# Decoder layer on one core: logits of two pairs of heads taken in one visit, in three places

## The chip, the cores and the metric

The kernel runs on one core of a Trainium2 chip. The engines are TensorE (PE in the profile), VectorE (DVE), ScalarE (ACT) and GpSimd (POOL); SyncE (SP) issues most of the DMAs. The metric is device time in microseconds, the median of several runs. All arithmetic that ends in the output is float32.

## The reference, cut to what matters

One layer of a decoder over 256 positions of width 1024. Three token mixers work side by side on projections of the same input, each with heads of 64:

```python
# A, 6 heads: sparse attention, one shared key and value; an indexer picks the top 64 keys of each query
logits = jnp.einsum('bqhd,bqkd->bqhk', qb, ksel) * scale + bias
# B, 3 groups x 4 slots: dilated windows; 3 query groups share a slot's keys, merged by their denominators
logits = jnp.einsum('bqhd,bqjhd->bqhj', qb[:, :, g], kg) * scale + bias
# C, 6 heads: block-sparse causal attention (with 256 positions: one causal block)
# all: softmax over the allowed keys, then the weighted sum of values
m = sum_b sigmoid(x @ Wg_b) * (o_b @ P_b)
x = LN(alpha * x + m @ w_out)
x = LN(alpha * x + relu(x @ w_up)**2 @ w_down + sigmoid(x @ w_ple_gate) * (p @ w_ple))
```

A table of relative-position biases is added to all logits.

## The kernel before

**Products.** A float32 product is made of three TensorE products of parts rounded to fp32r: high by high, high by low, low by high (`prod`, L184 to L192). Activations are split once; `xh` and `xl` are the parts of the input. Weights stream through `Weights` (L80 to L140): SP loads a unit into one of five `raw` buffers, ACT casts it to its high part `whi` (L112), DVE and POOL subtract to get the low part `wlo` (L123, each a share of the columns). Units are prepared four ahead of their use (`AHEAD`), in the order of the table `TASKS` (L44): a number is a feature tile, `g` a gate tile, `c` a merged output, `va` and `vb` the values, `a` and `o` what follows behind the mixers.

**Steps of the mixers.** `feat(f)` makes a tile of 128 projected features by 256 positions with 24 matmuls in one of three PSUM banks called `mm`; `q_pair` (ACT L285, DVE L286) and `k_pair` (L298, L299) read it, scale it and split it, which frees the bank. A tile of 128 features holds a pair of heads. `fill("g")` makes a gate tile in an `mm` bank, 24 matmuls, and ACT's tanh (L311, output `G`) frees the bank. `fill("c")` makes the merged output of mixers B and C for 128 columns with 15 matmuls from `op`, the heads' outputs (B gives its tiles 3 and 4, C its tiles 5 to 7), and three operations of DVE (L326, L326, L327) gate it and free the bank.

**Attention.** `logits` (L336 to L351) is one visit: for the two heads of a pair 12 matmuls with 64 rows, or 24 where a second pair rides along. Its results lie in the PSUM banks b0, b1, b2, taken in turn by `ps_s`; a 24-visit takes b3 too, through `ps_t`. `head` (L411 to L422) then does one head: DVE adds the bias (L416, output `e`, with the row minimum), ACT takes exp with the row sums (L419), DVE the reciprocal (L406), ACT the scaling by rows (L408, two instructions), and `attend` (L382 to L398) does the rest: three transposes on PE into b3 (L388), an ACT copy and a DVE subtraction into `pt` (L389, L390), two matmuls with the values into b4 (L392, L393), an ACT copy `ov` (L396) and two DVE additions (L397, L398). `pair_out` (ACT L401, DVE L402) splits a pair's output into `op`. `slots` does mixer B's pairs in the same manner, for three query groups at once.

**Order.** The mixers run as a series: two dilated pairs (`slots`, the first with a 24-visit for two of its three groups, the second with three 12-visits), three causal pairs (loop at L557), three query pairs of branch a (loop at L573, with the key `kA` shared by all heads), then what follows. Feature, gate and merged tiles stand between the heads. The scheduler writes one order for each engine from this program, and each engine executes its instructions strictly in that order; logits have a high priority in it (L341). The tiles for `e` come from the pool `wk` with three buffers, and branch a's masked bias `ta` (POOL, L584 and L585) from the same pool.

Of the kernel before, what the change touches and what calls it, by code (L numbers as in the profile page):

```python
# [11 lines left out]
F32 = mybir.dt.float32  # L12
# [28 lines left out]
DV = 640  # L41


TASKS = ("4 va 5 g 6 7 g 8 g g 9 g 10 11 g 12 g g vb g 13 14 g g 15 16 g g 17 18 g g "  # L44
         "19 g c 20 g c g c 21 g c g c g c g g g c c a a a a o o o o").split()


class Apart:
# [95 lines left out]
def hybrid_layer(ctx: ExitStack, tc: tile.TileContext, x0, xn, pT, wqk, wva, wvb, wg, wbc, wba,  # L144
# [188 lines left out]
            next(side, None)  # L333
        return ps

    def logits(k, *qs):  # L336


        ss = [next(ps_s if n < 3 else ps_t)[:, 0:384] for n in range(2 * len(qs))]
        with tc.high_priority(offset=500):  # L340
            for b in range(2):  # L341
                c = slice(b * 128, (b + 1) * 128)
                for n, q in enumerate(qs):
                    for i, (x, y) in enumerate(((1, 0), (0, 0), (0, 1))):
                        for h in (1, 0):
                            d = slice(64 * h, 64 * h + 64)
                            m = pe.matmul(ss[2 * n + h][:, QC[b]], lhsT=q[d, x, c],  # L347
                                          rhs=k[d, y, 0:128 * (b + 1)], start=i == 0, stop=i == 2)
# [59 lines left out]
            act.mul(P[:, QC[b]], P[:, QC[b]], r[:, b:b + 1])  # L408


    def head(s, t0, t1, vh, o, h):  # L411
        e = wk.tile([128, 384], F32, name="e", tag="e")
        mx = sm.tile([128, 2], F32, name="mx", tag="mx")
        den = sm.tile([128, 2], F32, name="den", tag="den")
        for b, t in enumerate((t0, t1)):
            dve.tensor_tensor_reduce(e[:, QC[b]], s[h][:, QC[b]], t, op0=ALU.add, op1=ALU.min,  # L416
                                     scale=1.0, scalar=-GONE, accum_out=mx[:, b:b + 1])
        for b in range(2):
            act.activation(e[:, QC[b]], e[:, QC[b]], AF.Exp, bias=mx[:, b:b + 1], scale=-1.0,  # L419
                           accum_out=den[:, b:b + 1])  # L420
        scale_rows(e, den)
        attend(e, vh, o, h)  # L422

    def slots(qs, k, Ts, vh, o, adds, two):

        es = [wk2.tile([128, 3, 384], F32, name="eb", tag="eb") for _ in range(2)]
        mxs = [sm.tile([128, 2, 3], F32, name="mxb", tag="mxb") for _ in range(2)]
        for g in range(3):

            if two and g == 0:  # L430
                s = logits(k, qs[1], qs[0])
                s, ss = s[2:], s[:2]
            else:
                s = ss if two and g == 1 else logits(k, qs[g])
# [33 lines left out]
    with ExitStack() as begin:  # L468
# [26 lines left out]
    tp, wk, wk2, sm = (right(n, b) for n, b in (("tp", 3), ("wk", 3), ("wk2", 2), ("sm", 6)))  # L495
    tab = bias_table()
    ps = feat(4)
    kI, kA = k_pair(ps[0:64], ps[0:64]), k_pair(ps[64:128], ps[64:128])
# [7 lines left out]

    values(u_va, 328, 0, 5, True)
    for j in range(4):
        s = s[2:] if j % 2 else logits(kI, iq[j], iq[j + 1])
# [23 lines left out]
    def opair():  # L533
        return wk2.tile([128, S], F32, name="o", tag="o")

    for j in range(2):
        ps = feat(5 + 4 * j)
        k = k_pair(ps)
        fill("g")
        qs = []  # L540
        for g in range(3):
            qs.append(q_pair(feat(6 + 4 * j + g)))
            if g:
                fill("g")
        o = opair()
        Ts = [toeplitz(6 + 2 * j + h, 4) for h in range(2)]
        slots(qs, k, Ts, 1 + 2 * j, o, (pool, dve)[j], j == 0)
        pair_out(o, 3 + j)
        banks_first[0] = True
        fill("g")  # L550
# [3 lines left out]
    dve.tensor_tensor(pl, pr, ph.bitcast(F32), op=ALU.subtract)  # L554
    values(u_vb, 384, 5, 6, False)
    fill("g")
    for j in range(3):  # L557
        ps = feat(13 + 2 * j)
        k = k_pair(ps)
        q = q_pair(feat(14 + 2 * j))  # L560
        s = logits(k, q)
        o = opair()
        for h in range(2):
            n = 2 * j + h
            if n % 3 == 0:
                T = toeplitz(18 + n, 1)
            head(s, T[:, n % 3, 128:256], T[:, n % 3], 5 + n, o, h)
            fill("g")
        pair_out(o, 5 + j)

    for _ in side:
        pass
    T = None  # L573
    q = q_pair(feat(19))
    for j in range(3):
        s = logits(kA, q)
        o = opair()
        for h in range(2):
            n = 2 * j + h
            if n % 3 == 0:  # L580
                T = toeplitz(n, 1)
            ta = wk.tile([128, 384], F32, name="ta", tag="ta")
            with tc.issue_after(W.subs[-3]):
                pool.tensor_tensor(ta[:, 0:128], T[:, n % 3, 128:256], am[:, 0:128], op=ALU.add)  # L584
                pool.tensor_tensor(ta[:, 128:384], T[:, n % 3], am[:, 128:384], op=ALU.add)  # L585
            head(s, ta[:, 0:128], ta[:, 128:384], 0, o, h)
            if h and j < 2:
                q = q_pair(feat(20 + j))
            fill("gc")
        pair_out(o, j)  # L590
    fill("gggcc")
    W.after = ()

# [532 lines left out]
```

## Time and profile before

| what | value |
|---|---|
| median of three runs | 429.45 us (429.26 to 430.65) |
| the profiled execution: its own time | 428.66 us |
| its span in the trace | 426.9 us |
| mean granted TensorE clock | 0.998 |
| 24-visits and 12-visits of the mixers at L347 | from 46 us to 165 us of the span |
| DVE busy, POOL busy | 82%, 28% |
| moved by DMA | 84.30 MB, 197 GB/s in the mean |

The span is what the trace covers; the execution's own time is 1.8 us longer. Times in rows of the trace count from the start of the span. In a row, `out<-in` names the tiles with their buffer numbers left out, and `x24` is the number of instructions in the group. The page cuts the span into 40 slices and gives each engine's busy share in tenths:

```profile
DVE  5968758898676689879967889989998798999755
ACT  6777385585888777858414668887888666567310
POOL 1668474173544556500010002242220000000001
```

A slice is 10.7 us; the mixers' attention fills slices 5 to 16. Busy shares of a slice say nothing of the order within it.

### The profile page before, as it was taken

What the parts mean: (1) busy time and instruction counts of PE and PEld (TensorE: products, weight loads), DVE (VectorE), ACT (ScalarE), POOL (GpSimd) and SP (SyncE); (2) the same over time, 40 slices, a digit from 0 to 9 for tenths busy, and PEclk for the clock granted to TensorE, in tenths of its full rate; (3) what the DMA queues carried; (4) which work ended last, traced back from release to release, by engine and by line L of the source; (5) the groups of instructions that cost most, each with busy time, mean ns of one, the idle gap of its engine ahead of it and who ended that gap; (6) DMA issues with size and microseconds to landing.
All of it is one profiled execution on the core that took longest, in us unless ns stands there. A gap on an engine that the chain in (4) does not pass through costs nothing.

```text
span 426.9 us, 7810 instructions
## 1 busy us (share of the span) xinstructions
PE 417.1 (98%) x2804; PEld 378.1 (89%) x2804; DVE 351.1 (82%) x645; ACT 279.6 (65%) x531; POOL 118.9 (28%) x127
## 2 busy tenths in 40 slices
PE   8999999999999999999999999999999999999993
PEld 8989999999999999999887888888888888788883
DVE  5968758898676689879967889989998798999755
ACT  6777385585888777858414668887888666567310
POOL 1668474173544556500010002242220000000001
PEclk9999999999999999999999999999999999999999
DMA  8895966567463327587851776785665376646402
GB/s 294 301 327 161 286 222 189 164 201 269 130 181 126 131 63 259 145 267 276 292 206 49 236 257 197 210 291 191 187 207 152 117 266 216 190 147 230 164 2 99
DMA packets 28157, 84.30 MB, mean 197 GB/s; under 512 B 2977, under 2 KB 6985, under 8 KB 27733
## 3 DMA queue, kind: packets, MB, share of 16 engines
q1 hardware_dynamic: 26880, 79.54, 57.0%
q10 hardware_dynamic: 1140, 4.19, 2.8%
q8 instruction: 22, 0.36, 0.4%
q14 instruction: 19, 0.15, 0.1%
q0 software_dynamic: 96, 0.06, 0.0%
HBM read 81.88 MB, written 1.90 MB: 196 GB/s over the span
## 4 chain that ended last, share of the span: by engine, by line
PE 78%; DVE 5%; DMA 4%; issue 2%; ACT 2%; SPq 0%; POOLq 0%; DVEq 0%; POOL 0%; ACTq 0%
PE mm L189 34%; PE b L189 19%; PE mm L891 14%; PE mm L893 7%; DMA xr<-in_wdn_dram 4%; PE b L347 2%; DVE wlo L119 2%; PE b L388 1%; PE b L392 1%; ACT whi L112 1%; DVE Y L853 1%; ACT ri L517 1%; PE b L393 0%; DVE wlo L123 0%; DVE st L701 0%
## 5 line engine op out<-in xcount | busy, mean ns | idle before, releaser
L112 ACT CAST whi<-raw 128x1024 fp32r<-128x1024 f32 (+3 forms) x92 | 89.9, 988 | 38.2 <-PE b L189 14.7
L123 DVE TENSOR_TENSOR wlo<-raw,whi 128x256 fp32r<-128x256 f32 (+3 forms) x118 | 96.4, 840 | 16.6 <-ACT whi L112 13.9
L189 PE MATMUL mm<-xh,whi 128*128 128x256 f32 x336 | 90.2, 280 | 0.0
L189 PE MATMUL mm<-xl,whi 128*128 128x256 f32 x336 | 88.1, 278 | 0.0
L123 POOL TENSOR_TENSOR wlo<-raw,whi 128x384 fp32r<-128x384 f32 (+1 forms) x50 | 68.4, 1377 | 70.2 <-ACT whi L112 65.5
L189 PE MATMUL mm<-xh,wlo 128*128 128x256 f32 x336 | 80.6, 281 | 0.2 <-DVE k L299 0.2
L189 PEld LDWEIGHTS mm<-xh,whi 128*128 128x128 f32 x336 | 63.1, 188 | 0.8
L891 PE MATMUL mm<-x,whi 128*128 128x512 f32 x256 | 63.4, 389 | 0.0
L189 PEld LDWEIGHTS mm<-xl,whi 128*128 128x128 f32 x336 | 63.1, 188 | 0.1
L189 PEld LDWEIGHTS mm<-xh,wlo 128*128 128x128 f32 x336 | 57.8, 188 | 0.8 <-DVE k L299 0.4
L189 PE MATMUL b<-whi,store 128*128 128x512 f32 x168 | 54.1, 389 | 0.0
L891 PEld LDWEIGHTS mm<-x,whi 128*128 128x128 f32 x256 | 45.7, 188 | 7.5
L119 DVE TENSOR_TENSOR wlo<-raw,whi 128x1024 fp32r<-128x1024 f32 (+2 forms) x38 | 43.2, 1159 | 3.7 <-ACT whi L112 3.6
L708 POOL TENSOR_TENSOR rs<-rs,half 128x1 f32<-128x1 f32 x4 | 3.4, 843 | 147.5 <-DVE rs L707 147.5
L110 ACT CAST whi<-raw 128x256 fp32r<-128x256 f32 x64 | 36.9, 617 | 10.0 <-PE mm L891 5.4
L189 PEld LDWEIGHTS b<-whi,store 128*128 128x128 f32 x168 | 31.5, 188 | 6.4
L893 PEld LDWEIGHTS mm<-x,wlo 128*128 128x128 f32 x256 | 33.8, 188 | 2.5
L893 PE MATMUL mm<-x,wlo 128*128 128x256 f32 x256 | 34.2, 276 | 0.0
L189 PE MATMUL b<-wlo,store 128*128 128x512 f32 x84 | 32.8, 391 | 0.3 <-DVE wlo L119 0.3
L914 POOL TENSOR_TENSOR a<-a 128x128 f32<-128x128 f32 x7 | 5.3, 757 | 61.5 <-ACT a L877 55.6
L189 PE MATMUL mm<-op,whi 128*128 128x256 f32 x128 | 22.4, 280 | 0.0
L189 PE MATMUL b<-whi,x 128*128 128x512 f32 x64 | 20.5, 395 | 0.0
(223 smaller groups left out, 824.2 us busy)
## 6 DMA issues: line engine op xcount, KB each, us to landing
raw<-in_wup_dram SPq DMA_DIRECT2D x32, 512.0 KB
raw<-in_wg_dram SPq DMA_DIRECT2D x24, 512.0 KB
raw<-in_wqk_dram SPq DMA_DIRECT2D x18, 512.0 KB
raw<-in_wdn_dram SPq DMA_DIRECT2D x18, 512.0 KB
raw<-in_wout_dram SPq DMA_DIRECT2D x8, 512.0 KB
raw<-in_wpg_dram SPq DMA_DIRECT2D x8, 512.0 KB
T<-tabd SPq DMA_DIRECT2D x24, 128.0 KB
xr<-in_wdn_dram SPq DMA_DIRECT2D x6, 512.0 KB
```

The source lines that it names most:

```text
L110: i = nc.scalar.copy(blocks(hi, a, b), blocks(r, a, b))
L112: i = nc.scalar.copy(hi, r)
L119: i = e.tensor_tensor(lo[:, x], r[:, x], hi[:, x].bitcast(F32), op=ALU.subtract)
L123: i = e.tensor_tensor(blocks(lo, *x), blocks(r, *x), blocks(hi, *x).bitcast(F32), op=ALU.subtract)
L189: i = pe.matmul(ps, lhsT=a[x], rhs=b[y], start=first and n == 0, stop=last and n == 2, skip_group_check=more)
L347: m = pe.matmul(ss[2 * n + h][:, QC[b]], lhsT=q[d, x, c], rhs=k[d, y, 0:128 * (b + 1)], start=i == 0, stop=i == 2)
L388: pe.transpose(t[:, 128 * i:128 * i + 128], P[:, 128 * i:128 * i + 128], ident)
L392: pe.matmul(v, lhsT=V[:, 0, vh], rhs=pt[:, :, 0:256], start=True, stop=False)
L517: act.mul(r[:, h, QC[0]], r[:, h, QC[0]], iw[:, 0, n:n + 1])
L891: pe.matmul(ps, lhsT=hi[:, c], rhs=x1[:, :, k], start=k == 0, stop=False)
L893: pe.matmul(ps[:, :, 0], lhsT=lo[:, c], rhs=x1[:, :, k, 0], start=False, stop=k == KT - 1)
L914: pool.tensor_tensor(sums[2], a11, a21, op=ALU.subtract)
```

## The change

Three pairs of visits become three visits:

- `logits` now takes (key, query) pairs, so that two pairs of heads with keys of their own can share a visit. In a 24-visit the second head of the first pair takes the bank of the transposes, b3.
- The second dilated pair is done as the first: two of its three query groups in one visit.
- The causal pairs run as (0, 1) and (2): both pairs' key and query tiles, features 13 to 16, are made first, then one visit of 24 follows, then the bias step of all four heads, then the four heads. `TASKS` puts the four gate tiles behind the four features.
- Branch a's query pairs run likewise as (0, 1) and (2): features 19 and 20 first. Feature 21 is made behind the fourth head.
- `head` is cut in two: `biased` (DVE's step) and `head` (everything from exp on). `wk` has four buffers; `ta` has a pool of its own, `wt`, with three.

The lines of the new kernel are shifted by some: the bias step is L415, exps are L422; matmuls of logits stay L347, scalings L408.

```diff
-TASKS = ("4 va 5 g 6 7 g 8 g g 9 g 10 11 g 12 g g vb g 13 14 g g 15 16 g g 17 18 g g "
-         "19 g c 20 g c g c 21 g c g c g c g g g c c a a a a o o o o").split()
+TASKS = ("4 va 5 g 6 7 g 8 g g 9 g 10 11 g 12 g g vb g 13 14 15 16 g g g g 17 18 g g "
+         "19 20 g c g c g c 21 g c g c g c g g g c c a a a a o o o o").split()
...
-    def logits(k, *qs):
+    def logits(*kqs):
-        ss = [next(ps_s if n < 3 else ps_t)[:, 0:384] for n in range(2 * len(qs))]
+        ss = [next(ps_t if n == 1 and len(kqs) == 2 else ps_s)[:, 0:384]
+              for n in range(2 * len(kqs))]
...
-    def head(s, t0, t1, vh, o, h):
+    def biased(s, t0, t1):
         e = wk.tile([128, 384], F32, name="e", tag="e")
         mx = sm.tile([128, 2], F32, name="mx", tag="mx")
+        for b, t in enumerate((t0, t1)):
+            dve.tensor_tensor_reduce(e[:, QC[b]], s[:, QC[b]], t, op0=ALU.add, op1=ALU.min,
+                                     scale=1.0, scalar=-GONE, accum_out=mx[:, b:b + 1])
+        return e, mx
+
+    def head(e, mx, vh, o, h):
         den = sm.tile([128, 2], F32, name="den", tag="den")
...
-        slots(qs, k, Ts, 1 + 2 * j, o, (pool, dve)[j], j == 0)
+        slots(qs, k, Ts, 1 + 2 * j, o, (pool, dve)[j], True)
...
-    q = q_pair(feat(19))
-    for j in range(3):
-        s = logits(kA, q)
-        o = opair()
-        for h in range(2):
-            n = 2 * j + h
+    qs = [q_pair(feat(19 + j)) for j in range(2)]
+    for js in ((0, 1), (2,)):
+        ems = []
+        ss = logits(*((kA, q) for q in qs[::-1]))
+        for i, s in enumerate(ss[-2:] + ss[:-2]):
+            n = 2 * js[0] + i
...
-            head(s, ta[:, 0:128], ta[:, 128:384], 0, o, h)
-            if h and j < 2:
-                q = q_pair(feat(20 + j))
+            ems.append(biased(s, ta[:, 0:128], ta[:, 128:384]))
+        for i, em in enumerate(ems):
+            n = 2 * js[0] + i
+            if n % 2 == 0:
+                o = opair()
+            head(*em, 0, o, n % 2)
+            if n == 3:
+                qs = [q_pair(feat(21))]
             fill("gc")
-        pair_out(o, j)
+            if n % 2:
+                pair_out(o, n // 2)
```

The causal loop is changed in the same way as branch a's. What the rows of each engine's order show of this follows at two places. In a row stands the line, the operation and the tiles with their numbers (the numbers differ between the two programs).

**The second dilated pair, on PE.** Before, the end of its second 12-visit and what follows it:

```order
L347 MATMUL b0_1227<-k_988,q_1062 128x256
L347 MATMUL b2_1226<-k_988,q_1062 128x256
L347 MATMUL b0_1227<-k_988,q_1062 128x256
L347 MATMUL b2_1226<-k_988,q_1062 128x256
L189 MATMUL mm_1106<-xh_112,wlo_954 128x256
```

Now, the end of a 24-visit, which works on two queries and four banks:

```order
L347 MATMUL b3_1230<-k_991,q_1106 128x128
L347 MATMUL b2_1229<-k_991,q_1106 128x128
L347 MATMUL b1_1232<-k_991,q_1065 128x128
L347 MATMUL b0_1231<-k_991,q_1065 128x128
L347 MATMUL b1_1232<-k_991,q_1065 128x128
L347 MATMUL b0_1231<-k_991,q_1065 128x128
```

Two queries, q_1106 and q_1065, share the key k_991 in one visit; feature and gate tiles no longer stand between the two.

**Branch a's first visit, on ACT.** Before, from the copy of a causal head's output `ov_2022` to the query `q_2317` of the second pair; `e_2175` and `e_2261` are the first pair's two heads:

```order
L396 COPY ov_2022<-b4_2019 64x512
L389 CAST pt1_116<-b3_2070 128x384
L419 ACTIVATE e_2175,den_2177<-e_2175,mx_2176 128x128
L419 ACTIVATE e_2175,den_2177<-e_2175,mx_2176 128x256
L419 ACTIVATE e_2261,den_2263<-e_2261,mx_2262 128x128
L419 ACTIVATE e_2261,den_2263<-e_2261,mx_2262 128x256
L408 ACTIVATE e_2175<-e_2175,r_2182 128x128
L408 ACTIVATE e_2175<-e_2175,r_2182 128x256
L408 ACTIVATE e_2261<-e_2261,r_2268 128x128
L408 ACTIVATE e_2261<-e_2261,r_2268 128x256
L112 CAST whi_2288<-raw_2286 128x640
L285 ACTIVATE q_2317<-mm_2285 128x256
```

Now, from the copy of a causal head's output `ov_2082` on; `e_2226` and `e_2233` are the first pair's heads, `e_2240` and `e_2251` the second's:

```order
L396 COPY ov_2082<-b4_2079 64x512
L422 ACTIVATE e_2226,den_2256<-e_2226,mx_2227 128x128
L422 ACTIVATE e_2226,den_2256<-e_2226,mx_2227 128x256
L422 ACTIVATE e_2233,den_2335<-e_2233,mx_2234 128x128
L422 ACTIVATE e_2233,den_2335<-e_2233,mx_2234 128x256
L422 ACTIVATE e_2240,den_2417<-e_2240,mx_2241 128x128
L422 ACTIVATE e_2240,den_2417<-e_2240,mx_2241 128x256
L422 ACTIVATE e_2251,den_2496<-e_2251,mx_2252 128x128
L408 ACTIVATE e_2226<-e_2226,r_2259 128x128
L408 ACTIVATE e_2226<-e_2226,r_2259 128x256
L112 CAST whi_2390<-raw_2388 128x1024
L311 ACTIVATE G_114<-mm_2437 128x256
```

Seven exps of four heads stand together where four of two heads stood, ahead of the first scaling. The weight cast `whi_2390` and the tanh of the gate tile `mm_2437` stand behind the first head's scaling.

**The same place, on PE.** Now, behind the gate tile `mm_2437` come the first head's transposes and a merged output `mm_2477`:

```order
L189 MATMUL mm_2437<-xh_112,wlo_2280 128x256
L388 MATMUL b3_2263<-ident_75,e_2226 128x128 x3
L189 MATMUL mm_2477<-op_129,whi_2311 128x256 x2
L189 MATMUL mm_2477<-op_129,wlo_2312 128x256 x2
L189 MATMUL mm_2477<-op_129,whi_2311 128x256 x4
L189 MATMUL mm_2477<-op_129,wlo_2312 128x256
```

Its last matmuls, with those of two other merged outputs, wait for the causal pairs' last output; then come the product with V of the first head, the second head's transposes, and the feature tile `mm_2516`:

```order
L189 MATMUL mm_2477<-op_129,whi_2311 128x256
L189 MATMUL mm_2477<-op_129,wlo_2312 128x256
L392 MATMUL b4_2269<-pt0_115,V_126 128x512
L393 MATMUL b4_2269<-pt0_115,V_126 128x2x128
L388 MATMUL b3_2342<-ident_75,e_2233 128x128 x3
L189 MATMUL mm_2516<-xh_112,wlo_2359 128x256
```

Before, the first head's transposes stood among the 24 matmuls of a gate tile, and a 12-visit and a feature tile stood close by; now they stand behind a whole gate tile and ahead of a merged output.

**The same place, on DVE.** Before, from the subtraction for `pt` of the first pair's second head to two weight parts:

```order
L390 TENSOR_TENSOR pt1_116<-b3_2272,pt1_116 128x384
L326 SCALAR_TENSOR_TENSOR mm_2239<-G_114,mm_2239 128x256
L398 TENSOR_TENSOR o_2167<-ov_2195 64x256
L326 SCALAR_TENSOR_TENSOR mm_2360<-G_114,mm_2360 128x256
L326 SCALAR_TENSOR_TENSOR G_114<-G_114,mm_2239 128x256
L326 SCALAR_TENSOR_TENSOR G_114<-G_114,mm_2360 128x256
L327 TENSOR_TENSOR G_114<-G_114,mm_2239 128x256
L123 TENSOR_TENSOR wlo_2289<-raw_2286,whi_2288 128x3x128
L123 TENSOR_TENSOR wlo_2324<-raw_2321,whi_2323 128x5x128
```

Now, from the subtraction of the first pair's first head:

```order
L390 TENSOR_TENSOR pt0_115<-b3_2263,pt0_115 128x384
L326 SCALAR_TENSOR_TENSOR mm_2316<-G_114,mm_2316 128x256
L326 SCALAR_TENSOR_TENSOR mm_2395<-G_114,mm_2395 128x256
L326 SCALAR_TENSOR_TENSOR G_114<-G_114,mm_2316 128x256
L326 SCALAR_TENSOR_TENSOR mm_2477<-G_114,mm_2477 128x256
L326 SCALAR_TENSOR_TENSOR G_114<-G_114,mm_2395 128x256
L327 TENSOR_TENSOR G_114<-G_114,mm_2316 128x256
L123 TENSOR_TENSOR wlo_2359<-raw_2356,whi_2358 128x5x128
L123 TENSOR_TENSOR wlo_2391<-raw_2388,whi_2390 128x5x128
```

The same number of operations stands between the subtraction and the first weight part `wlo`; three merged outputs are gated there in place of two, and the weight part is that of the feature tile `mm_2516`.

More of the change, by code (lines that the diff above doesn't have):

```diff
@@ L342, in logits @@
                 c = slice(b * 128, (b + 1) * 128)
-                for n, q in enumerate(qs):
+                for n, (k, q) in enumerate(kqs):
                     for i, (x, y) in enumerate(((1, 0), (0, 0), (0, 1))):
@@ L408, in scale_rows @@
             act.mul(P[:, QC[b]], P[:, QC[b]], r[:, b:b + 1])
-    def head(s, t0, t1, vh, o, h):
+    def biased(s, t0, t1):
         e = wk.tile([128, 384], F32, name="e", tag="e")
         mx = sm.tile([128, 2], F32, name="mx", tag="mx")
+        for b, t in enumerate((t0, t1)):
[3 more added lines that the diff above has]
+    def head(e, mx, vh, o, h):
         den = sm.tile([128, 2], F32, name="den", tag="den")
-        for b, t in enumerate((t0, t1)):
-            dve.tensor_tensor_reduce(e[:, QC[b]], s[h][:, QC[b]], t, op0=ALU.add, op1=ALU.min,
-                                     scale=1.0, scalar=-GONE, accum_out=mx[:, b:b + 1])
         for b in range(2):
@@ L430, in slots @@
             if two and g == 0:
-                s = logits(k, qs[1], qs[0])
+                s = logits((k, qs[1]), (k, qs[0]))
                 s, ss = s[2:], s[:2]
             else:
-                s = ss if two and g == 1 else logits(k, qs[g])
+                s = ss if two and g == 1 else logits((k, qs[g]))
             for h in range(2):
@@ L494, in hybrid_layer @@
         iq = [q_pair(ps, 0.125) for ps in first]
-    tp, wk, wk2, sm = (right(n, b) for n, b in (("tp", 3), ("wk", 3), ("wk2", 2), ("sm", 6)))
+    tp, wt, wk, wk2, sm = (right(n, b) for n, b in (("tp", 3), ("wt", 3), ("wk", 4), ("wk2", 2),
+                                                    ("sm", 6)))
     tab = bias_table()
@@ L508, in hybrid_layer @@
     for j in range(4):
-        s = s[2:] if j % 2 else logits(kI, iq[j], iq[j + 1])
+        s = s[2:] if j % 2 else logits((kI, iq[j]), (kI, iq[j + 1]))
         r = wk2.tile([128, 768], F32, name="ri", tag="eb")
@@ L556, in hybrid_layer @@
     fill("g")
-    for j in range(3):
[L558 to L561, printed above, removed]
-        o = opair()
-        for h in range(2):
-            n = 2 * j + h
+    for js in ((0, 1), (2,)):
+        kqs = []
+        for j in js:
+            ps = feat(13 + 2 * j)
+            kqs.append((k_pair(ps), q_pair(feat(14 + 2 * j))))
+        ems = []
+        ss = logits(*kqs[::-1])
+        for i, s in enumerate(ss[-2:] + ss[:-2]):
+            n = 2 * js[0] + i
             if n % 3 == 0:
                 T = toeplitz(18 + n, 1)
-            head(s, T[:, n % 3, 128:256], T[:, n % 3], 5 + n, o, h)
+            ems.append(biased(s, T[:, n % 3, 128:256], T[:, n % 3]))
+        for i, em in enumerate(ems):
+            n = 2 * js[0] + i
+            if n % 2 == 0:
+                o = opair()
+            head(*em, 5 + n, o, n % 2)
             fill("g")
-        pair_out(o, 5 + j)
+            if n % 2:
+                pair_out(o, 5 + n // 2)
     for _ in side:
@@ L573, in hybrid_layer @@
     T = None
-    q = q_pair(feat(19))
-    for j in range(3):
-        s = logits(kA, q)
-        o = opair()
-        for h in range(2):
-            n = 2 * j + h
+    qs = [q_pair(feat(19 + j)) for j in range(2)]
+    for js in ((0, 1), (2,)):
+        ems = []
+        ss = logits(*((kA, q) for q in qs[::-1]))
+        for i, s in enumerate(ss[-2:] + ss[:-2]):
+            n = 2 * js[0] + i
             if n % 3 == 0:
                 T = toeplitz(n, 1)
-            ta = wk.tile([128, 384], F32, name="ta", tag="ta")
+            ta = wt.tile([128, 384], F32, name="ta", tag="ta")
             with tc.issue_after(W.subs[-3]):
@@ L585, in hybrid_layer @@
                 pool.tensor_tensor(ta[:, 128:384], T[:, n % 3], am[:, 128:384], op=ALU.add)
-            head(s, ta[:, 0:128], ta[:, 128:384], 0, o, h)
-            if h and j < 2:
-                q = q_pair(feat(20 + j))
+            ems.append(biased(s, ta[:, 0:128], ta[:, 128:384]))
+        for i, em in enumerate(ems):
+            n = 2 * js[0] + i
+            if n % 2 == 0:
+                o = opair()
+            head(*em, 0, o, n % 2)
+            if n == 3:
+                qs = [q_pair(feat(21))]
             fill("gc")
-        pair_out(o, j)
+            if n % 2:
+                pair_out(o, n // 2)
     fill("gggcc")
```

## The prediction

> **What bounds the kernel now.** I read the busy times at the page's head first, then the shares of the chain that ended last, then PE's waits (each row: total, times, longest), then that chain in order of time where it leaves PE.
>
> ```profile
> PE 417.1 (98%) x2804; PEld 378.1 (89%) x2804; DVE 351.1 (82%) x645; ACT 279.6 (65%) x531; POOL 118.9 (28%) x127
> PE 78%; DVE 5%; DMA 4%; issue 2%; ACT 2%; SPq 0%; POOLq 0%; DVEq 0%; POOL 0%; ACTq 0%
> PE b L189 <- DVE wlo L119: 0.3, 1, 0.3
> PE mm L189 <- DVE wlo L123: 0.3, 1, 0.3
> ```
>
> PE is busy for 98% of the span, the chain runs on it for 78%, and once it has begun no wait of PE that is put down to another engine is longer than 0.3 us. A matmul taken off PE there is therefore worth its whole time, and a wait put in front of PE costs its whole time. Later stages that wait for DMA don't take it up either, as far as I can follow them: their loads are issued when PE frees the buffers, so they move with it. The one wait of 0.3 us "mm L189 <- DVE wlo L123" is the place to look at. The chain in order of time shows what leads to it, in branch a:
>
> ```profile
> 148.88 1.05 ACT whi L112
> 149.93 0.28 ACT G L311
> 150.21 0.29 ACT op L401
> 150.50 0.90 ACT e L419 x4
> ...
> 156.12 0.56 DVE wlo L123
> 156.68 0.04 issue
> 156.72 6.55 PE mm L189 x55
> ```
>
> For 7.8 us, from 148.88 to 156.68, the chain is off PE: ACT casts a weight, takes a gate's tanh, does a pair's output and a head's exps, then DVE adds, merges and subtracts. PE works through all of it on matmuls it had in store and comes out 0.3 us short. So branch a already runs with no margin between PE and its side engines, and it is there that the change puts more side work ahead of PE.
>
> **The visits.** Each of the three merges makes one visit of 24 small matmuls out of two of 12. The trace holds both kinds, each between the same kind of neighbours:
>
> ```profile
> 53.31 0.39 PE L189 MATMUL mm<-xh,wlo 128*128 128x256 f32 x2
> 53.63 0.95 PE L347 MATMUL b<-k,q 64*128 64x128 f32 x12
> 54.52 0.38 PE L189 MATMUL mm<-xh,whi 128*128 128x256 f32 x1
> 54.74 0.28 PE L189 MATMUL mm<-xl,whi 128*128 128x256 f32 x1
> ```
>
> ```profile
> 46.07 0.39 PE L189 MATMUL mm<-xh,wlo 128*128 128x256 f32 x2
> 46.39 1.64 PE L347 MATMUL b<-k,q 64*128 64x128 f32 x24
> 47.96 0.39 PE L189 MATMUL mm<-xh,whi 128*128 128x256 f32 x1
> 48.19 0.28 PE L189 MATMUL mm<-xl,whi 128*128 128x256 f32 x1
> ```
>
> ```profile
> 183.36 14.70 PE mm L189 x129
> ```
>
> A full matmul takes 14.70/129 = 0.114 us. From 53.31 to 54.74 are 1.43 us with three such matmuls beside the visit: the 12 cost 1.43 - 0.34 = 1.09. From 46.07 to 48.19 likewise, 2.12 - 0.34 = 1.78 for 24. Merging saves 2 x 1.09 - 1.78 = 0.40 us, three times 1.2 us. The number of small matmuls is the same; what goes is the price of entering and leaving a visit. Where a visit stood between transposes some of that price stays, so I keep 0.9 as the term's lower end. No DMA is added or removed, and every matmul, exp and copy stands in both kernels; the rest is order.
>
> **Branch a's first visit, replayed.** Behind the 24-visit the new order puts on ACT: the copy of a head's output, seven exps, the first head's two scalings, a cast, a gate's tanh, one exp, op, four more scalings, and the copy of the first transposes. On PE: one head's product with V, 24 matmuls, the three transposes of the first head, 12 + 9 matmuls of merged outputs, V, three transposes, and 24 of a feature. Each engine goes strictly in that order. Count time from the end of the visit, and take durations from here:
>
> ```profile
> 144.55 1.48 ACT L408 ACTIVATE e<-e,r 128x128 f32<-128x128 f32 x4
> 145.94 0.71 ACT L112 CAST whi<-raw 128x640 fp32r<-128x640 f32 x1
> ```
>
> ```profile
> 149.83 0.38 ACT L311 ACTIVATE G<-mm 128x256 f32<-128x256 f32 x1
> 150.11 0.40 ACT L401 CAST op<-o 128x256 fp32r<-128x256 f32 x1
> ...
> 153.06 0.48 ACT L389 CAST pt<-b 128x384 fp32r<-128x384 f32 x1
> ```
>
> ```profile
> 182.85 0.40 PE L392 MATMUL b<-pt,V 128*128 128x512 f32 x1
> ...
> 183.08 0.28 PE L393 MATMUL b<-pt,V 128*128 128x256 f32 x1
> ...
> 183.40 0.58 ACT L396 COPY ov<-b 64x512 f32<-64x512 f32 x1 [1.68 <-PE b L393]
> ```
>
> ```profile
> 153.67 0.54 DVE L390 TENSOR_TENSOR pt<-b,pt 128x384 fp32r<-128x384 f32 x1
> ...
> 156.12 2.02 DVE L123 TENSOR_TENSOR wlo<-raw,whi 128x384 fp32r<-128x384 f32 x3
> 141.03 0.83 DVE L123 TENSOR_TENSOR wlo<-raw,whi 128x640 fp32r<-128x640 f32 x1 [0.85 <-ACT whi L112]
> 70.35 0.33 PE b L388 x3
> ```
>
> A head's two exps with their sums take 0.90 (the chain above, x4), so seven exps 3.1; four scalings take 145.94 - 144.55 = 1.39, so two 0.70. The cast's pitch is 149.83 - 148.88 = 0.95, tanh's and op's 0.28 and 0.29 (the chain). A product with V takes 183.08 - 182.85 = 0.23 of PE and another 0.114, three transposes 0.33.
> 1. PE reaches the first transposes at 0.35 + 24 x 0.114 = 3.1. ACT starts the copy 0.55 after the product with V begins (183.40 - 182.85), ends it at 1.15, the exps at 4.25, the two scalings at 4.95, say 5.0. **PE waits 1.9.**
> 2. Of the three matmul banks two are held by merged outputs that lack the third causal pair's op, the third by the gate tile just made. The next 12 matmuls need its tanh, behind the cast: 5.0 + 0.95 + 0.38, in all about 6.25, where PE alone would have been at 3.4. **Late by 2.8**, the 1.9 included.
> 3. op comes at 7.0, its low half at 7.5: in time for the last nine. PE ends the 21 at 6.25 + 2.4 = 8.65. ACT, after exp, op and four scalings, copies the transposes at 8.3 to 8.8, DVE subtracts to 9.35, and only then V can go: **0.7 more**. PE leaves V and transposes at 10.0.
> 4. On DVE six operations stand between that subtract and the weight's low half, as many of the same kinds as in the rows above, where it took 156.12 - 153.67 = 2.45 from start to start: 8.8 + 2.45 + 0.83 = 12.1. The feature's first matmul needs that half: **2.1 more**.
>
> PE without waits would stand there at 3.1 + 0.33 + 2.4 + 0.35 + 0.33 = 6.5. The stall is 12.1 - 6.5 = 5.6 us. Its lower end allows each of the four links 0.2 less, since these rows give each step only once or twice: 4.9. Its upper end takes the low half at 1.56 us, as DVE has it when POOL works beside it, in place of 0.83, and some pitch more: 6.5.
>
> ```profile
> 67.25 1.56 DVE L123 TENSOR_TENSOR wlo<-raw,whi 128x640 fp32r<-128x640 f32 x1
> ```
>
> What the stall replaces is the old wait of 0.3, which goes. Behind it the weights that PE needs have been prepared during its idle time, and I find no second stall. The other two merges have cover: in the dilated pair the transposes come over 10 us behind the visit; in the causal pairs PE has about 70 matmuls, 8 us, between the visit and the first transposes, against 4 x 0.90 + 2 x 1.39 = 6.4 if all four heads' exps and scalings came first, which is close but enough. If that cover failed, each us missing there would be added. The fourth bank costs nothing: the bank of the transposes is lent to one head's logits, which DVE reads (0.27 to 0.42 an instruction, two for a head) well before the first transposes need it.
>
> **Sum.** -1.2 - 0.3 + 5.6 = +4.1 on the profiled execution of 428.66 us, that is 432.7. The median of the runs is 429.45, 0.8 above it; the same step gives 429.45 + 4.1 = **433.5**. Ends: 429.45 - 1.5 + 4.9 = 432.9 with all links fast, and 429.45 - 0.9 - 0.3 + 6.5 = 434.8 with all slow and the visits saving least.
>
> **The rivals.**
> - The stall does not occur and only the visits count: 429.45 - 1.5 = 427.9, faster. It is decided at one place: whether the first head's scaled exps are there within 3.1 us of the visit's end. For it: PE has hidden a side chain of 7.8 us before. Against: for those 7.8 us PE had matmuls in store; now 24 and a product with V stand ahead of the transposes, and ACT has 1.15 + 3.1 + 0.7 to do. 0.09.
> - Only the first link bites: the tanh's bank or the op is not needed as I read it, PE catches up with weights in store, and 1.9 of waiting stands against the 1.5 gained: 429.45 + 0.4 = 429.8, no change. 0.10.
> - The clock falls. In the 9 us from the first wait to the last PE works only about 3.4.
>
> ```profile
> 200.00:230.00 30.00, 30.00 (x136) 24.26 (x135) 23.65 (x37) 11.73 (x19) 1.56 (x2) 1.00 0.55 194
> 421.00:426.90 5.90, 0.00 (x0) 0.00 (x0) 2.34 (x4) 0.00 (x0) 0.94 (x1) 0.83 0.24 89
> ```
>
> The third number from the end is the granted clock. With no matmul at all for 5.9 us its mean is 0.83: if it fell to a half, it fell after 3.9 us (5.9 x (1 - 2 x 0.17)). My longest single wait is 2.0, so I expect 1.00 throughout. If it did halve for half of those 3.4 us of matmuls, they take 1.7 more: 433.5 + 1.7 = 435.2. 0.06. [...]
> - A second stall behind the first, since ACT still has eight scalings and casts to do: each head's exps and scalings are 1.6 (0.90 + 0.70), and one head late costs up to that and a link more: 436. 0.05.
>
> **How the numbers follow.** The forecast 433.5 (own range 431.0 to 434.8: from a stall of 3.0, in which two of the four links fail to add up, to one of 6.5) has 0.70, the four rivals 0.30. For eight in ten the range reaches down to 429.7, so that it holds the case in which only the first link bites, and up to 435.2, the halved clock; left out are the first and the last rival, 0.14. About 0.3% is what a measurement of this kernel can tell from no change, 1.3 us: faster 0.09, same 0.10 (429.8 lies in it), slower 0.81.
>
> **What would show it.** In the new profile PE should wait for "ACT e" (scaling) before the first transposes of branch a, for "ACT G" before the merged output, for "DVE pt" before V and for "DVE wlo" before a feature, of 1.9, 0.9, 0.7 and 2.1 us, all within 12 us of one visit; the three visits should be x24 with 1.6 us each; nothing of the kind should stand in the causal pairs. PE's busy time should fall by 1.2 and its share by more. I am wrong if PE's waits there sum to under 3 us, if ACT's seven exps do not stand ahead of the scalings on the chip, or if a wait of over 1 us appears at the causal or dilated visit.

## The result and the profile after

The changed kernel takes 434.74 us (median of four runs, 433.91 to 437.11) against 429.36 for the kernel before: a ratio of 1.0131 (95% interval 1.0106 to 1.0157; the medians alone give 1.0125). It is 5.4 us slower; 4.1 were forecast. Its profiled execution took 434.19 us, its span is 432.4. The ratio of each experiment is to the kernel before, run beside it; one of e1's twelve executions took 1081.76 us, and its ratio leaves that one out.

The page's busy times and shares of the chain, and the longest waits of PE, of the changed kernel:

```profile
PE 419.3 (97%) x2804; PEld 380.3 (88%) x2804; DVE 350.4 (81%) x645; ACT 279.9 (65%) x531; POOL 118.7 (27%) x127
PE 82%; DVE 4%; issue 3%; ACT 3%; POOLq 0%; DVEq 0%; POOL 0%; ACTq 0%
```

```profile
PE mm L189 <- DVE wlo L123: 1.6, 1, 1.6
PE b L388 <- ACT e L408: 1.2, 1, 1.2
PE mm L189 <- ACT G L311: 0.9, 1, 0.9
```

These are three waits of PE of a size that the kernel before did not have, one each, and all three stand within 13 us behind branch a's 24-visit, as the chain in order of time shows (start, length, what):

```profile
148.83 1.57 PE b L347 x24
...
150.96 2.65 PE mm L189 x23
153.61 0.03 ACTq L112
153.63 0.97 ACT e L422 x6
154.60 0.69 ACT e L408 x2
155.29 0.94 ACT whi L112
156.23 0.03 issue
156.25 0.38 ACT G L311
...
158.81 0.37 ACT pt L389
159.18 0.02 issue
159.21 0.56 DVE pt L390
159.77 0.85 DVE mm L326 x2
160.61 0.33 DVE G L326
...
161.85 1.36 DVE wlo L123
163.20 0.04 issue
163.25 1.79 PE mm L189 x13
```

The reader sees the steps of the prediction in their order: exps, scalings, cast, tanh, the copy and subtraction for `pt`, the gating, the weight's low half. PE resumes at 163.25, which is 12.85 us behind the visit's end at 150.40; without waits it would have stood there 6.5 behind it. The stall is 6.4 us. The three waits make 3.7 of it; in the rest PE works more slowly than at full pace, in good part at half clock (granted 0.50 from 157.91 to 161.32 us, below), while the chain runs over ACT and DVE.

PE's busy time rose by 2.2 us, though each visit became cheaper. Two things hide in it. The first is the start. Both programs begin alike, yet in the second from 5 to 6 us PE finished 10 matmuls in the profile of before and 6 in that of the changed kernel (columns: stretch, its length, PE busy and count, clock, DMA share, GB/s):

```profile
5.00:6.00 1.00, 1.00 (x10) 1.00 1.02 187
```

```profile
5.00:6.00 1.00, 1.00 (x6) 1.00 0.92 252
```

The clock's column reads 1.00 in both, but the trace's records of the clock begin only at 5.05 and at 7.72 us; the pace is read from the counts. PE worked at half pace to about 5 us in the one and to about 7.7 us in the other, so that its 60th matmul came 1.20 us later, ahead of anything that was changed. The second is a stretch of half clock inside the stall, of which more below.

The n-th matmul of PE in each profile, against the n-th in that of before, shows where time is lost or gained (us later; worked out from the starts of all matmuls; the 1150th stands just ahead of branch a's visits in before, the 1500th in its last third; since the orders differ, 0.1 to 0.2 hangs on which matmul is taken). Runs are named as in the experiments that follow:

| kernel | 60th | 1150th | 1500th | last |
|---|---|---|---|---|
| changed | 1.20 | 0.00 | 5.71 | 5.53 |
| changed, again (e11) | 0.93 | -0.28 | 5.98 | 6.03 |
| dilated visit alone (e1) | 1.15 | 1.70 | 1.51 | 1.50 |
| causal visit alone (e2) | 0.54 | 0.55 | 2.73 | 1.92 |
| both, without branch a (e12) | 1.27 | 0.21 | 2.46 | 1.79 |
| branch a's visit alone (e3) | 0.57 | 0.45 | 2.56 | 7.05 |
| merged outputs late, exps held (e8) | 1.40 | 0.33 | -0.40 | 5.83 |
| three links shorter (e9) | 1.24 | -0.04 | 4.76 | 4.55 |

From the 60th to the 1150th matmul the changed kernel gains 1.20 us with two merged visits, from there to the 1500th it loses 5.71, and later it gains 0.18. Counted from the 60th matmul, that is without the start, it is 4.33 us later than before.

### The profile page after: what moved, and what is told of

Its sections match the earlier page's. It is cut to its first block, busy times and chain, and to the rows that moved or that the text cites. A ratio compares the mean times of both kernels' runs of the same rounds, so it can differ in the third digit from the quotient of the medians.

```text
span 432.4 us, 7807 instructions
## 1 busy us (share of the span) xinstructions
PE 419.3 (97%) x2804; PEld 380.3 (88%) x2804; DVE 350.4 (81%) x645; ACT 279.9 (65%) x531; POOL 118.7 (27%) x127
## 4 chain that ended last, share of the span: by engine, by line
PE 82%; DVE 4%; issue 3%; ACT 3%; POOLq 0%; DVEq 0%; POOL 0%; ACTq 0%
PE mm L189 34%; PE b L189 23%; PE mm L908 13%; PE mm L910 7%; PE b L347 2%; PE b L388 1%; PE b L392 1%; DVE wlo L123 1%; DVE store L119 1%; DVE G L678 1%; ACT whi L112 1%; ACT ri L521 1%; DVE G L679 0%; ACT e L408 0%; PE b L393 0%
## 5 line engine op out<-in xcount | busy, mean ns | idle before, releaser
L189 PE MATMUL mm<-op,whi 128*128 128x256 f32 x128 | 23.3, 287 | 0.9 <-ACT G L311 0.9
L189 PEld LDWEIGHTS mm<-op,whi 128*128 128x128 f32 x128 | 19.5, 196 | 1.3 <-ACT G L311 1.1
```

Of the source, the lines that this page charges most:

```text
L189: i = pe.matmul(ps, lhsT=a[x], rhs=b[y], start=first and n == 0, stop=last and n == 2, skip_group_check=more)
```

## The experiments

### Each merge by itself (e1, e2, e3, e12)

e1 is the kernel before with one argument changed:

```diff
-        slots(qs, k, Ts, 1 + 2 * j, o, (pool, dve)[j], j == 0)
+        slots(qs, k, Ts, 1 + 2 * j, o, (pool, dve)[j], True)
```

> The kernel before with the second dilated pair's 24-visit alone. My sum: one merge saves 0.4 us on PE and nothing waits for it, 429.4 - 0.4 = 429.0; between the two profiles the same matmuls come 0.9 us sooner across this place, so 428.5 if all of that is this visit. Rival, that a merged visit saves PE nothing: 429.4.

Measured: 430.10 us against 429.17, ratio 1.0017 (1.0005 to 1.0028). Neither theory: slightly slower. The table has the reason in rough: 0.55 lost between the 60th and the 1150th matmul. In the profile the visit itself gives its part back (0.28 less from the 540th to the 660th matmul), and later, at 103 us, stands a wait of 0.4 us at a product with V for DVE's subtraction for `pt`, which before hasn't; what took the rest stays open. The run is no clean test of the merge either: in its order on PE, 6 of the visit's 24 matmuls stand at 71.7 us and the other 18 at 76.2, with 32 matmuls of other tiles between, whereas the changed kernel has all 24 together at 76.2.

e2, e3 and e12 are the changed kernel with loops and `TASKS` of before put back: in e2 for branch a and the dilated pair, in e3 for the causal and the dilated pairs, in e12 for branch a alone. Buffers stay as in the changed kernel. For e2 and e12 branch a's loop is again

```diff
-    for js in ((0, 1), (2,)):
-        ems = []
-        ss = logits(*((kA, q) for q in qs[::-1]))
+    for j in range(3):
+        s = logits((kA, q))
...
+            head(*biased(s[h], ta[:, 0:128], ta[:, 128:384]), 0, o, h)
+            if h and j < 2:
+                q = q_pair(feat(20 + j))
             fill("gc")
```

> The causal pairs' merge alone; dilated pairs and branch a as before. My sum: 0.4 us saved, the cover of 8 us ahead of the first transposes suffices, 429.0 (428.6 to 429.2). Rival, that the four heads' exps reach PE here too: a wait of PE for ACT e behind the 24-visit, and 430 or more.

Measured: 430.57 us, ratio 1.0038 (1.0022 to 1.0054). Slower, but not for the rival's reason: no wait for ACT stands behind the causal visit. The loss of 2.2 us is in branch a, whose code is that of before, at a product with V that waits 1.9 for DVE's subtraction. The visit's gain doesn't show in the table (0.54, then 0.55): as in e1, PE loses time near 103 us, with a wait of 0.16 at a product with V.

> The changed kernel with branch a as before: only the dilated and the causal visits are merged. If the parts added up, e1 and e2 would make it 0.9 + 1.4 slower: 431.5. My theory, that each order has one place with too little cover in branch a, makes it like e2, with one wait of about 2 us at a V product there, less 0.4 for the dilated visit: 430 to 431. Rival, that these two merges gain where branch a's is left out: 428.4.

Measured: 430.45 us, ratio 1.0030 (1.0011 to 1.0049), in the forecast range. The two visits gain 1.06 us by the 1150th matmul and then one wait in branch a takes 1.9. Waits of PE and the chain at that place, of e12:

```profile
PE b L392 <- DVE pt L390: 1.9, 1, 1.9
```

```profile
155.75 0.76 DVE mm L326 x2
156.52 0.32 DVE G L326
156.84 0.59 DVE ov L397
157.43 0.33 DVE G L326
157.76 0.48 DVE pt L390
158.24 0.04 issue
158.28 0.50 PE b L392
```

Ahead of the subtraction that PE waits for, DVE gates two merged outputs (L326). They had been held until the third causal pair's `op` came. So the kernel before has no margin at this place, and the causal merge ahead of it is enough to tip it over: e2 has the same wait of 1.9, though it came to branch a no sooner than before. The dilated merge alone isn't enough: e1 loses nothing between the 1150th and the 1500th matmul (1.70, then 1.51).

> Branch a's merge alone; dilated and causal pairs as before. My theory, that the whole loss is the chain behind this one visit: the changed kernel's 434.7 without the other two gains of 0.4 to 0.9 each, 435.5 to 436.5. Rival, that the loss is spread over the three merges or comes from the start of the program: under 433.

Measured: 436.41 us, ratio 1.0159 (1.0144 to 1.0174), within the forecast. The place is only half of what I meant: the stall behind the visit is 2.1 us in this order, and 4.5 more are lost behind the 1500th matmul. PE's waits in e3:

```profile
PE mm L189 <- ACT G L311: 2.7, 2, 1.5
PE mm L189 <- ACT op L401: 2.1, 1, 2.1
```

The wait for `op` stands at 194 us, where the last pair of branch a is late, and the clock is halved right behind it, from 195.81 to 199.22 us, which by estimate takes up to half of those 3.41 us more. The parts do not add up: without the start (last column less the first) they are 0.35, 1.38 and 6.48, in all 8.2, where the whole change has 4.33. Each order has waits of its own.

### The links of the stall (e4, e6, e9, e10)

e4 holds each head's exps in branch a behind the scaling of the head before:

```diff
+        with ExitStack() as held:
+            if hold is not None:
+                held.enter_context(tc.issue_after(hold))
-        for b in range(2):
-            act.activation(e[:, QC[b]], e[:, QC[b]], AF.Exp, bias=mx[:, b:b + 1], scale=-1.0,
+            for b in range(2):
+                act.activation(e[:, QC[b]], e[:, QC[b]], AF.Exp, bias=mx[:, b:b + 1], scale=-1.0,
...
-            head(*em, 0, o, n % 2)
+            done = head(*em, 0, o, n % 2, done if n else None)
```

> The changed kernel with one order changed on ACT: in branch a each head's exps are issued behind the scaling of the head before. PE's order stays as it is up to 12 us behind the visit. Theory of four links in a row: the first wait (ACT e before the transposes, 1.2 us) goes, but the reciprocals of heads three and four, which now wait for later exps, stand on DVE ahead of the gating and of the weight part that PE waits for, so the end of the chain stays within 1 us of where it was: 434 to 435.5. Rival, that seven exps ahead of the first scaling are the whole cause: the time falls by the wait of 1.2 and the 0.9 behind it or more, 432.6 or less.

Measured: 436.18 us, ratio 1.0145 (1.0126 to 1.0163): no faster than the change, a little above the range. The wait for ACT e is gone from the list, and PE waits 1.8 for the tanh and 2.5 for the low half in its place. So the rival falls: exps ahead of the scaling are not by themselves the price. My reason is not shown either. The chain there runs over PE, which takes 3.81 us for the merged outputs' matmuls (x17 in that view; 2.25 in e9 at full clock) at half clock, and the reciprocals wait beside it. PE resumes with the feature at 163.36 us, 13.35 behind the visit's end. A second stretch of half clock, 162.88 to 166.30 us, then falls on the feature and takes by estimate about 1.5 us, which the expectation had no place for.

e6 issues the gating of the second and third merged output behind the low half of feature 21's weight:

```diff
+            with ExitStack() as held:
+                if f in (1, 2):
+                    held.enter_context(tc.issue_after(W.dsubs[u_q[21][0]]))
                 for i, o in ((1, ps[:, 1]), (0, g[:, 0])):
...
```

> The changed kernel with one order changed on DVE: of the six gating operations between the subtraction for pt and the low half of feature 21's weight, the three that belong to the second and third merged output are issued behind that low half. PE's order is unchanged up to that feature. Theory that this DVE chain is the last link: the low half is there 1.0 us sooner, and 433.7 to 434.2 results, since PE is then held by V's transposes at half pace and by the second V product. Rival, that the stall ends elsewhere (clock, bank, op): 434.7.

Measured: 434.60 us, ratio 1.0117 (1.0100 to 1.0135), which reads like the rival's number. The chain of e6 says otherwise:

```profile
160.38 0.98 DVE wlo L124
161.36 0.04 issue
161.40 4.63 PE mm L191 x24
```

The visit of e6 ended at 149.78, so PE resumes 11.6 us behind it, 1.2 sooner than in the changed kernel, as the link's price said. But the 24 matmuls that follow take 4.63 us where 24 x 0.114 = 2.7 is their full pace: the half clock (granted 0.50 from 161.50 to 164.91) now falls behind the stall, and most of the 1.9 too many is by estimate its doing (half of 3.41 us is 1.7).

e9 joins e4's and e6's orders and puts the reciprocals of heads three and four, and with them their scalings, behind the same weight (shown against e4's code):

```diff
+        with ExitStack() as held:
+            if late:
+                held.enter_context(tc.issue_after(W.dsubs[u_q[21][0]]))
-        i = scale_rows(e, den)
+            i = scale_rows(e, den)
```

> The changed kernel with the ACT order of e4, the DVE order of e6, and the reciprocals of heads three and four behind feature 21's weight part, which in e4 stood in the way. PE's order is unchanged up to 12 us behind the visit. By the durations of the rows the feature's low half is then there 9.6 us behind the visit in place of 12.8, so 434.7 - 3.3 = 431.4 (430.8 to 432.4, the upper end with a stretch of halved clock that the shorter stall no longer hides). Rival, that the order of these side steps doesn't set the stall: 434 or more.

Measured: 434.01 us, ratio 1.0115 (1.0089 to 1.0141): only a part. PE resumes at 160.63, 10.3 behind the visit's end at 150.32, so the first stall is 2.5 us shorter where 3.2 were forecast. Then come two waits that it did not have before (waits of PE in e9 of over 0.2 us, less that at the program's start):

```profile
PE mm L191 <- ACT G L313: 1.8, 1, 1.8
...
PE mm L191 <- DVE wlo L124: 1.1, 1, 1.1
PE mm L191 <- DVE G L332: 0.8, 1, 0.8
PE b L397 <- DVE pt L395: 0.4, 1, 0.4
```

What was moved behind the weight part (gating, and with it the freeing of a bank, and the next `pt`) is late for the next user: 0.8 and 0.4. Without the start, e9 is 3.31 us later than before, the changed kernel 4.33 and 5.10 in its two profiles.

e10 also takes the gate's tanh ahead of the weight cast, by preparing that weight later:

```diff
-                gemm(ps, u_g[n_g[0]], xs)
-                freed(act.activation(G[:, n_g[0]], ps, AF.Tanh, scale=0.5))
+                gemm(ps, u_g[n_g[0]], xs, ahead=AHEAD - 2 * (n_c[0] == 2))
+                i = act.activation(G[:, n_g[0]], ps, AF.Tanh, scale=0.5)
+                freed(i)
+                tanh[0] = i.ins if n_c[0] == 2 else None
...
-            hi, lo = W.get(u_bc[f][0])
+            hi, lo = W.get(u_bc[f][0], AHEAD - (f == 1), tanh[0] if f == 2 else None)
```

> As the run before, and the gate's tanh, which frees the bank, stands ahead of the weight cast on ACT (that cast is issued later). The second link then shrinks by 0.95, but on DVE two more low halves come to stand ahead of the second head's subtraction: 0.9 less at the merged output, 0.85 at the feature, and a new wait of some 2 us at the second V product, in all 431.5 to 433. Rival, that the bank's wait is the dominant link: 430 or less.

Measured: 433.40 us, ratio 1.0098 (1.0083 to 1.0113). That is a little above the range. The wait for the tanh is 0.8 (1.8 in e9) and the one at the second V product 2.3, as forecast; but the feature begins 10.2 us behind the visit, as in e9 (10.3), and not 0.85 sooner, after waits of 0.3 for `op` and 1.3 for the low half. So the first, second and fourth link are waits that can be shortened or taken away, and each time part of the gain is lost at a later step.

### The merged outputs later (e7, e8)

e7 puts two gate tiles behind the first two heads and the merged outputs later; e8 holds the exps as well, as e4:

```diff
-         "19 20 g c g c g c 21 g c g c g c g g g c c a a a a o o o o").split()
+         "19 20 g g g g g c 21 c c g c c c g g g c c a a a a o o o o").split()
...
-            fill("gc")
+            fill(('gg', 'gg', 'gc', 'cc', 'gc', 'cc')[n])
```

> The changed kernel with branch a's fills in another order: two gate tiles behind each of the first two heads in place of a gate and a merged output each, the merged outputs later. Then no mm bank is held by a merged output that lacks the third causal pair, and PE has 39 matmuls and more between the visit and the first transposes. The seven exps ahead of the scaling stay. Theory of the links: the first two vanish, one wait remains where a merged output needs a bank whose gating stands behind the heads' scalings, about 1.4 us: 429.0 to 430.5. Rival, that exps ahead of the scaling are the cause by themselves: 433 or more.

> Both: merged outputs late as in the run before, and each head's exps behind the scaling of the head before. No engine then has to wait for a chain behind the visit by the durations of the trace: the before's 429.2 less 1.2 for the visits and 0.3 for the old wait, 427.7 (427.3 to 428.6). Rival, that a 24-visit in branch a costs time whatever stands behind it: 430 or more.

Measured: 434.32 us for e7 (ratio 1.0113, 1.0087 to 1.0139) and 434.58 for e8 (1.0118, 1.0074 to 1.0161). Both expectations of the time fail; what they say of the first stall holds. In e7 one wait of 1.6 us is left of it, for the gating of a merged output (1.4 expected). At the 1500th matmul e8 is 0.40 us ahead of before, 1.8 with the start taken out: up to there neither the visit nor anything behind it costs time. The time is lost at the mixers' end. Waits of PE in e7, then in e8:

```profile
PE mm L189 <- DVE G L327: 4.0, 2, 2.4
```

```profile
PE mm L189 <- DVE G L327: 3.0, 2, 2.1
```

The merged outputs, moved back, crowd there with the last heads: PE waits for DVE's gating to free a bank, at 192 us for 2.4 and at 193 us for 2.1. In e8 the clock is halved right behind that wait (granted 0.50 from 194.75 to 198.16 us): the 20 matmuls there take 3.98 us, and 2.91 in e7, where the clock stays full (mean granted clock 0.997). The mean granted clock of e8's four executions orders their times too: 432.53 us at 0.997, 434.66 and 434.49 at 0.993, 436.37 at 0.987.

### The clock (e5, e11)

e5 fills PE's first wait with transposes of the identity that nothing reads:

```diff
-        t = next(ps_t)[:, 0:384]
+        t = next(ps_t)
+        for i in range(12 if vh == 0 and n_pt[0] == 11 else 0):
+            pin(pe.transpose(t[:, 384:512], ident, ident))
+        t = t[:, 0:384]
```

> The changed kernel with 12 transposes of the identity, into columns that nothing reads, ahead of the first transposes of branch a, where PE waits 1.4 us. They add work and leave none out. Theory that the chain over ACT and DVE sets the end of the stall and the halved clock inside it is hidden: 434.5 to 435.2, no gain although the clock there should stay at 1.00 for longer. Rival, that the clock's fall is part of the price: the 12 or so matmuls at half pace are worth 1.3 us, and the time falls to 433.4.

Measured: 435.32 us, ratio 1.0134 (1.0116 to 1.0153): no gain, and just above the range. The clock stays full through most of the stall and falls to 0.50 near its end, at 161.5 us, for 6.8 us. The merged outputs' 17 matmuls run at full pace here (2.25 us), and still PE resumes 12.85 us behind the visit's end, just as in the changed kernel's first profile. So the halved clock inside that profile's stall hardly set its length. What the whole kernel would take at full clock throughout is not shown, since here the fall comes behind the stall: 40 matmuls take 7.68 us there.

e11 is the changed kernel once more.

> The changed kernel once more, for a second profile of the same program. The stall should end 12.8 us behind the visit again, within 0.2. What may differ is where the stretch of 3.4 us at half clock falls: inside the stall again (then 434 to 434.7), or behind it (then up to 1.7 more), and when the clock becomes full at the start (4.5 to 7.7 us in the profiles so far, up to 1.2 us of time). Rival, that the clock has no part in the spread from 433.9 to 437.1: the same places and the same spread.

Measured: 435.26 us (434.44 to 436.70), ratio 1.0142 (1.0118 to 1.0166). PE resumes 13.4 us behind the visit (12.85 in the first profile), so the 0.2 that I allowed were too few. Windows of the first profile of the changed kernel, then of e11 (stretch, length, busy time and count of PE, PEld, DVE, ACT and POOL, then the clock):

```profile
154.50:157.91 3.41, 1.99 (x13) 1.56 (x14) 0.59 (x2) 3.38 (x11) 1.00 (x1) 1.00 0.00 0
157.91:161.32 3.41, 3.41 (x17) 3.31 (x17) 2.11 (x6) 3.41 (x8) 0.74 (x1) 0.50 0.00 0
```

```profile
152.78:156.19 3.41, 1.41 (x9) 0.78 (x7) 1.21 (x8) 3.39 (x12) 0.17 (x1) 1.00 0.00 0
156.19:159.61 3.42, 3.21 (x15) 3.21 (x16) 1.15 (x3) 3.40 (x11) 0.83 (x1) 0.50 0.00 0
```

In both the clock is halved for 3.41 us, right behind a stretch of 3.41 us in which PE was busy for 1.99 and 1.41. In the first it falls late, and the chain runs over ACT and DVE beside it: it costs nothing that can be seen. In e11 it falls on the merged outputs from their first matmul, and the chain runs over PE:

```profile
156.41 3.72 PE mm L189 x17
```

At full clock the same matmuls take 2.25 (e9). DVE then comes to the weight's low half 0.6 us later than in the first profile, counted from the visit's end (12.0 against 11.45). So the clock's price in one and the same program depends on where the stretch falls: about nothing here, 0.5 there, up to 1.9 where it falls behind the stall (e6), by estimate 3.1 where it lasts 6.8 us (e5: 7.68 us for 40 matmuls, 40 x 0.114 = 4.56 at full pace). That this makes the spread up to 437.11 is not shown, since that execution was not profiled; its mean granted clock is 0.988, and those of the other three are 0.990 and 0.991.

## Why the prediction was right

The time of 434.74 lies in the stated range, between the forecast of 433.5 and the case of the halved clock.

- **What bounds the kernel**: right. PE had no margin at branch a's begin, and e2 and e12 show it most plainly: with branch a's code as before, a causal merge ahead of it brings a wait of 1.9 in it.
- **The visits, 0.40 each**: right in sign and too small. Two merges gave 1.20 us by the 1150th matmul, 0.6 each. Alone they gave nothing by the 1150th (e1, e2), where PE waited for a side chain near 103 us; the dilated visit of e1 was torn besides.
- **First link, a wait of 1.9 at the transposes**: measured 1.2. The exps began and ended as forecast; the first transpose needs only the first of the two scalings, so that it began 4.55 us behind the visit and not 5.0.
- **Second link, merged output at 6.25 behind the visit**: measured 6.3 (156.69 against 150.40).
- **Third link, V at 9.35 with a wait of 0.7**: DVE's subtraction ended at 9.37, but V came at 9.97 and did not wait for it, since PE worked at half clock then (granted 0.50 to 161.32 us). So this link was not one of the waits.
- **Fourth link, the low half at 12.1**: measured 12.8. The six gating operations began as forecast and took 0.2 longer, and the subtraction took 1.36 us, not 0.83. This is the term that was mis-sized: the stall is 6.4 where the sum had 5.6. I had 1.56 as the upper end, for POOL at work beside DVE; but POOL worked beside the row of 0.83 too. What differs is who began first. There DVE began at 141.03, and it was POOL's subtraction that took long; in the row of 1.56 (from 67.25) POOL's had begun at 67.11, and in the stall POOL was first again:

```profile
141.07 1.65 POOL L123 TENSOR_TENSOR wlo<-raw,whi 128x384 fp32r<-128x384 f32 x1 [0.29 <-ACT whi L112]
```

```profile
161.51 2.27 POOL L123 TENSOR_TENSOR wlo<-raw,whi 128x384 fp32r<-128x384 f32 x2 [0.21 <-ACT whi L112]
161.85 2.62 DVE L123 TENSOR_TENSOR wlo<-raw,whi 128x640 fp32r<-128x640 f32 x2
```

- **The signs**: PE's waits were to be 1.9, 0.9, 0.7 and 2.1, in all 5.6; they were 1.2, 0.9, none and 1.6, in all 3.7, still above the 3 that would have shown me wrong. PE's busy time was to fall by 1.2 us and rose by 2.2, for the start and the half clock.
- **Causal pairs and dilated pair without a wait**: right for the changed kernel.
- **The sum**: +4.1 forecast, +4.33 in the first profile and +5.10 in the second with the start taken out of both. That +4.33 comes so near is in part luck: the stall was 0.8 longer, and the visits and the steps behind them made up for most of it. (Four links of 0.2 less make a lower end of 4.8, not 4.9; nothing hangs on it.) The medians differ by 5.4. Between the first profiles the rest, 1.20, is the start; between the medians it is not shown, though the start, where the profile of before was an early one (its 428.66 us against a median of 429.36), and the clock are likely.
- **The clock at 1.00 throughout**: wrong. The step that failed is the one from a longest wait of 2.0 us to no fall: the clock fell in both profiles of the changed kernel, behind waits of at most 1.24 us. That the first of these falls cost nothing is luck. I had given this case 0.06.

No version tried beats the kernel before.

## What to carry to other kernels

A merge that saves work on the bounding engine is to be priced by what it puts in the queue ahead of the next thing that engine needs: here 0.6 us saved per visit met 6.4 us of exps, gating and weight parts that came due at once. Such a chain could be worked out here from the order of each engine and the durations of the profile before, each wait and each point in time of it to within 0.7 us. Where there was no margin, moving work within a queue mostly moved the wait, and the parts of the change didn't add up.

## What the runs showed of the hardware

Ahead of the program's last microseconds the granted clock fell in seven of the fourteen profiles (the changed kernel, e3, e4, e5, e6, e8 and e11), for stretches of 3.41 us (granted 0.50 from 157.91 to 161.32 in the changed kernel) or, in e5, of twice that (161.51 to 168.34). In the changed kernel the clock was at 1.00 for 150.19 us ahead of the fall, 44.0 times the length of the fall. In the 3.41 us at full clock just ahead of a fall PE was busy for 1.12 us (e8), 1.25 (e5), 1.41 (e11), 1.75 (e6) and 1.99 (the changed kernel). In other stretches of 3.41 us, counted from a change of the clock on, it was busy for 1.76 (e9), 1.95 and 2.28 (e7) and 2.47 (e6), and full clock followed. So PE's busy time alone doesn't part the cases: half clock followed 1.99, and full clock followed 1.76. The longest wait told no more: in e10 PE waited 2.3 us at one place and the clock stayed full ahead of the program's end (mean granted clock 0.994), while in the changed kernel it fell behind waits of at most 1.24. Windows of e6 and e9:

```profile
158.09:161.50 3.41, 1.75 (x13) 1.28 (x11) 2.85 (x6) 3.39 (x8) 1.34 (x2) 1.00 0.00 0
161.50:164.91 3.41, 3.41 (x16) 3.41 (x17) 3.41 (x7) 1.02 (x2) 3.41 (x5) 0.50 0.58 167
```

```profile
154.55:157.96 3.41, 1.76 (x15) 1.76 (x16) 1.26 (x3) 3.38 (x11) 1.00 (x1) 1.00 0.00 0
```

At the start, full pace began between 4.5 and 7.8 us in the fourteen profiles. That alone doesn't set how late the 60th matmul is: in e6 full pace began at 4.49 us, sooner than before (5.05), and yet that matmul came 0.57 later; PE had waited 0.36 us for ACT's `sh` just ahead of 8 us, as it did in six others for 0.2 to 0.4. In all the 60th matmul came up to 1.4 us later than in the profile of before (e8), and two profiles of one program, of the changed kernel and e11, differ by 0.27 there.

The 128x640 subtraction of DVE that ends the stall lasted longer the more was left of a POOL subtraction that had begun before it. In the changed kernel, e4, e5, e6, e10 and e11, POOL's had from 0.37 to 0.77 us left when DVE's began, and DVE's took that and 0.68 us more in each, 1.05 to 1.45 us; at 141.03 us before, where POOL's began second, DVE's took 0.83.
